# The fourth open PSUM bank of a wide output projection: drawn from the mixers' pool instead of the transposes' pool

## The chip, the cores and the metric

The kernel runs on one core of one Trainium2 chip. The metric is device time in microseconds (us) of one execution. Every time given here comes from the runs of the kernel or from one execution taken with the hardware profiler.

## What is computed

Two layers of a hybrid block over 1024 tokens of width 1024. Each layer normalises its input, projects it into four mixers (a pooling mixer, retention, a spatial gate, a gated delta rule), projects their joined output back, adds the residual, and then runs a convolutional feed-forward part of inner width 2816:

```python
h = rms_norm(x, g_pre_mix)
p = h @ w_in
...
y = jnp.concatenate([y_a, y_b, y_c, y_d], axis=-1).astype(dt)
x = x + rms_norm(y @ w_out, g_post_mix)
h = rms_norm(x, g_pre_ffn)
x = x + rms_norm(conv_ffn(h, ffn_w_up, ffn_conv_w, ffn_conv_b, ffn_w_down), g_post_ffn)
```

The change touches the product `y @ w_out`, the output projection, in three of its four executions.

## The kernel before

**Tiling.** The 1024 tokens are worked off in two halves of 512 (h = 0 and 1), each as four blocks of 128 tokens. Every float32 weight unit (128 x 1024) is loaded on SP's queue into one of two `raw` buffers, rounded to a high part on ScalarE (L183, `whi`) and the remainder taken on VectorE or GpSimd (L184, `wlo`); `whi` and `wlo` have three buffers each. A product is then three TensorE matmuls: high x high, high x low, low x high.

**Order of the stages.** `run` writes them down as: feed-forward of layer 0 half 0, its norms, the transposes of the result (`to_hT`), the output projection of layer 0 half 1 (`out(0, 1)`), the input projection and mixers of layer 1 half 0 (`win(1, 0)`), and so on; one step later the same sequence comes again with `out(1, 0)` and `win(1, 1)`. The third call of the wide projection, `out(1, 1)`, is put into the middle of the feed-forward part of layer 1 half 0 (`mid`). A scheduler then orders the instructions of each engine; every engine works off its own list strictly in that order, and waits on semaphores of the others.

**The wide projection.** `k_outer` (L219 to L234) keeps four PSUM banks open, one per token block b, and runs over the eight weight units `wO` in two column halves q of four units each: for each unit, for each block, two inner steps of three matmuls (L230, L231, L232). So one call of `out` makes 2 x 4 x 4 x 2 x 3 = 192 matmuls of 128x512. After the last unit of a half, ScalarE copies each bank out (L994).

**The PSUM pools.** The eight banks are split into three pools: `psg`, three banks, for the large products; `psh`, two banks, for the transposes of `to_hT` (L363, eight of 128x128 per token block, four to a bank); `psm`, three banks, for the mixers' small products. A pool hands its banks out in the order in which the program text asks for them, and a new tenant waits until the one before it has been read. `k_outer` asks for three banks of `psg` and one of `psh`. In both places where `to_hT(acc)` stands ahead of `out` in `run`, all eight `psh` tenants of the transposes come before the fourth bank of `k_outer`.

**What feeds the transposes.** `norms` (L308 to L320) goes over the four blocks of `acc`: a sum of squares on ScalarE (L305), an inverse root of ten small VectorE steps (L293, L276 to L284), a scaling (L315), the residual added (L316, `xb`, with two buffers, stored by L317 and loaded by L312 on SP's queue), a second sum of squares and inverse root, and a second scaling (L320), whose result is transposed on TensorE (L363) and split into `hT` by ScalarE (L366) and VectorE (L367). `hT` is what `win` multiplies by: its first matmuls are L214 to L216.

Of the kernel before, what the change touches and what calls it, by code (L numbers as in the profile page):

```python
# [115 lines left out]
class Net:  # L116
# [100 lines left out]
            yield b, ps  # L217

    def k_outer(self, aps, hT, kpu):  # L219
        banks = [self.ps(), self.ps(), self.ps(), self.pq("h")]  # L220
        nk = len(hT)
        for i, ap in enumerate(aps):
            hi, lo = self.unit(ap)
            for b in range(NB):
                tb = slice(b * P, b * P + P)
                for kk in range(kpu):
                    k = kpu * i + kk
                    s = slice(kk * 512, kk * 512 + 512)
                    h0, h1 = hT[k][0][:, tb], hT[k][1][:, tb]
                    self.nc.tensor.matmul(banks[b], h0, hi[:, s], start=k == 0, stop=False)  # L230
                    self.nc.tensor.matmul(banks[b], h0, lo[:, s], start=False, stop=False)  # L231
                    self.nc.tensor.matmul(banks[b], h1, hi[:, s], start=False, stop=k == nk - 1)  # L232
                if i == len(aps) - 1:
                    yield b, banks[b]  # L234
# [943 lines left out]
```

## Time and profile before

| what | value |
|---|---|
| median of 3 runs | 2557.17 us (2554.63 to 2559.59) |
| the profiled execution | 2563.22 us, of which its span is 2561.4 us |
| mean granted TensorE clock | 0.979 |
| VectorE busy | 1723.7 us (67%) |
| ScalarE busy | 937.4 us (37%) |
| GpSimd busy | 237.3 us (9%) |
| data moved | 265.54 MB, a mean of 104 GB/s |

The profile's page gives, for one execution, each engine's busy time, a strip of 40 time slices, the chain of work that ended last, and the costliest groups of instructions by source line. Behind it stands the trace, from which single instructions, waits and windows of time are read. PE is TensorE, PEld its weight loads, DVE VectorE, ACT ScalarE, POOL GpSimd, SP the queue that issues most transfers. PEclk is the granted TensorE clock as a share of full speed. A row of the timeline gives start, duration, engine, line, operation, output and input tiles and their count, and in brackets how long the engine stood idle before it and what ended the wait. Matmuls overlap: one of 128x512 is shown with some 0.39 us, but the next starts earlier, and the distance between two starts is what a matmul costs in a dense stretch.

### The profile page before, as it was taken

The numbers are of one execution on the slowest core, as the hardware profiler recorded it, in microseconds if no ns is written. First come the engines' busy times: TensorE is split into PE (matmuls) and PEld (weight loads), VectorE is DVE, ScalarE is ACT, GpSimd is POOL, SyncE is SP. The second block draws the span as 40 slices with busy tenths as digits, with TensorE's granted clock in tenths as the row PEclk, the third lists the DMA queues.
The fourth block names the chain that finished last, engine by engine and source line by source line (L and its number), as shares of the span: only waits on it lengthen the run. The fifth ranks groups of instructions, "written<-read, shape, count | busy, mean of one in ns | idle before, by whom it ended". The sixth has DMA issues, their size and how long they took to land.

```text
span 2561.4 us, 35079 instructions
## 1 busy us (share of the span) xinstructions
PE 2450.8 (96%) x13532; PEld 1998.9 (78%) x13532; DVE 1723.7 (67%) x3553; ACT 937.4 (37%) x1382; POOL 237.3 (9%) x318
## 2 busy tenths in 40 slices
PE   8999898999999799799999979989999999999998
PEld 7878677877788588687778858878777888888886
DVE  8895689765655768966565576896556476655556
ACT  6343452432333345243233334524323243432332
POOL 2321113000000012300000000230000000000001
PEclk9999999999999799999999979999999999999999
DMA  5233342322233343222222334322223244433322
GB/s 182 72 96 109 120 134 85 97 83 75 79 99 117 129 142 116 71 80 87 80 83 92 115 123 147 120 75 80 87 80 99 91 156 139 134 98 99 99 92 90
DMA packets 94651, 265.54 MB, mean 104 GB/s; under 512 B 30146, under 2 KB 30466, under 8 KB 93972
## 3 DMA queue, kind: packets, MB, share of 16 engines
q1 hardware_dynamic: 90564, 251.17, 30.8%
q0 software_dynamic: 3344, 11.08, 1.3%
q8 instruction: 107, 1.75, 0.3%
q10 hardware_dynamic: 576, 1.05, 0.1%
q14 instruction: 60, 0.49, 0.1%
HBM read 241.20 MB, written 22.05 MB: 103 GB/s over the span
## 4 chain that ended last, share of the span: by engine, by line
PE 82%; DVE 12%; issue 3%; ACT 2%; DMA 1%; POOL 1%; SPq 0%; DVEq 0%; POOLq 0%; ACTq 0%
PE psg L194 16%; PE psg L195 16%; PE psg L193 15%; PE psg L1016 6%; PE psg L1017 6%; PE psg L1018 6%; DVE pr L830 3%; PE psg L214 1%; PE psg L215 1%; PE psg L216 1%; DVE A L832 1%; PE psg L230 1%; PE psg L232 1%; PE psg L231 1%; DVE wlo L184 1%
## 5 line engine op out<-in xcount | busy, mean ns | idle before, releaser
L194 PE MATMUL psg<-hT,whi 128*128 128x512 f32 x1856 | 739.5, 398 | 1.8 <-DVE hT L367 1.8
L195 PE MATMUL psg<-hT,wlo 128*128 128x512 f32 x1856 | 738.7, 400 | 0.0
L193 PE MATMUL psg<-hT,whi 128*128 128x512 f32 x1856 | 731.2, 394 | 1.5 <-ACT tmp L430 1.4
L183 ACT CAST whi<-raw 128x1024 fp32r<-128x1024 f32 (+1 forms) x383 | 397.9, 1048 | 858.3 <-PE psg L194 340.8
L184 DVE TENSOR_TENSOR wlo<-raw,whi 128x1024 fp32r<-128x1024 f32 (+1 forms) x360 | 440.1, 1230 | 304.7 <-ACT whi L183 297.6
L193 PEld LDWEIGHTS psg<-hT,whi 128*128 128x128 f32 x1856 | 353.7, 191 | 82.6 <-issue 2.0
L194 PEld LDWEIGHTS psg<-hT,whi 128*128 128x128 f32 x1856 | 350.0, 189 | 83.7 <-DVE hT L367 2.9
L195 PEld LDWEIGHTS psg<-hT,wlo 128*128 128x128 f32 x1856 | 349.8, 188 | 76.1 <-issue 1.2
L1023 DVE TENSOR_TENSOR acc<-acc,psg 128x512 f32<-128x512 f32 x312 | 212.6, 685 | 138.3 <-PE psg L1018 137.0
L1016 PE MATMUL psg<-whi,g 128*128 128x512 f32 x696 | 277.3, 400 | 0.3 <-DVE acc L1023 0.3
L1017 PE MATMUL psg<-wlo,g 128*128 128x512 f32 x696 | 274.1, 394 | 0.0
L1018 PE MATMUL psg<-whi,g 128*128 128x512 f32 x696 | 273.4, 393 | 0.0
L1016 PEld LDWEIGHTS psg<-whi,g 128*128 128x128 f32 x696 | 130.7, 188 | 31.4 <-DVE acc L1023 1.6
L1018 PEld LDWEIGHTS psg<-whi,g 128*128 128x128 f32 x696 | 130.8, 188 | 30.2
L215 PE MATMUL psg<-wlo,hT 128*128 128x256 f32 (+1 forms) x512 | 147.4, 289 | 6.1 <-DVE wlo L184 6.1
L1048 DVE TENSOR_TENSOR c<-c,psg 128x512 f32<-128x512 f32 x88 | 60.5, 688 | 136.6 <-PE psg L195 128.5
L1017 PEld LDWEIGHTS psg<-wlo,g 128*128 128x128 f32 x696 | 130.9, 188 | 27.2 <-DVE c L1048 0.2
L214 PE MATMUL psg<-whi,hT 128*128 128x256 f32 (+1 forms) x512 | 146.4, 288 | 3.7 <-DVE rqk L508 3.4
L216 PE MATMUL psg<-whi,hT 128*128 128x256 f32 (+1 forms) x512 | 146.6, 287 | 0.0
L830 DVE SCALAR_TENSOR_TENSOR pr<-A 64x1 f32<-64x1 f32 (+30 forms) x124 | 113.0, 912 | 7.9 <-POOL A L826 5.6
L1047 ACT ACTIVATE c<-c 128x512 f32<-128x512 f32 x88 | 55.6, 632 | 168.5 <-DVE c L1046 85.8
L215 PEld LDWEIGHTS psg<-wlo,hT 128*128 128x128 f32 x512 | 97.4, 190 | 10.0 <-DVE wlo L184 7.1
(393 smaller groups left out, 3064.7 us busy)
## 6 DMA issues: line engine op xcount, KB each, us to landing
raw<-in_wU SPq DMA_DIRECT2D x176, 512.0 KB, 3.5
raw<-in_wD SPq DMA_DIRECT2D x88, 512.0 KB, 3.6
raw<-in_wA SPq DMA_DIRECT2D x56, 512.0 KB, 3.6
raw<-in_wO SPq DMA_DIRECT2D x32, 512.0 KB, 3.6
raw<-in_wB SPq DMA_DIRECT2D x24, 512.0 KB, 3.5
xs<-xb SPq DMA_DIRECT2D x24, 512.0 KB, 2.8
xb<-xs SPq DMA_DIRECT2D x20, 512.0 KB, 3.6
raw<-in_wS SPq DMA_DIRECT2D x8, 528.0 KB, 3.5
```

Of the source, the lines that this page charges most:

```text
L183: nc.scalar.copy(hi[:, :n], raw[:, :n])
L184: eng.tensor_tensor(lo[:, :n], raw[:, :n], hi[:, :n].bitcast(F32), ALU.subtract)
L193: nc.tensor.matmul(ps, a[0], b[0], start=first, stop=False)
L194: nc.tensor.matmul(ps, a[0], b[1], start=False, stop=False)
L195: nc.tensor.matmul(ps, a[1], b[0], start=False, stop=last)
L215: self.nc.tensor.matmul(ps[:, :width], h0, lo[:, s], start=False, stop=False)
L216: self.nc.tensor.matmul(ps[:, :width], h1, hi[:, s], start=False, stop=k == len(hT) - 1)
L830: V.scalar_tensor_tensor(pr[:, 0:i, 0:i], A[:, 0:i, 0:i], -1.0, A[:, 0:i, i].unsqueeze(1).to_broadcast([64, i, i]), ALU.mult, ALU.mult)
L1016: nc.tensor.matmul(ps, hi[:, tb], us[i][0][:, s], start=i == 0, stop=False)
L1017: nc.tensor.matmul(ps, hi[:, tb], us[i][1][:, s], start=False, stop=False)
L1018: nc.tensor.matmul(ps, lo[:, tb], us[i][0][:, s], start=False, stop=i == len(g0) - 1)
L1023: V.tensor_tensor(acc[b][:, s], acc[b][:, s], ps, ALU.add)
```

## The change

The call that asks for the fourth bank of `k_outer` gets it from `psm` instead of `psh`:

```diff
     def k_outer(self, aps, hT, kpu):
-        banks = [self.ps(), self.ps(), self.ps(), self.pq("h")]
+        banks = [self.ps(), self.ps(), self.ps(), self.pq()]
         nk = len(hT)
         for i, ap in enumerate(aps):
             hi, lo = self.unit(ap)
```

No instruction is added to or removed from the computation; the fourth bank's tenants change, and with them the order in which the scheduler puts the instructions.

**TensorE, first of the two places (`to_hT(acc)` and `out(0, 1)`).** Before, the transposes of all four token blocks (`acc_5206` to `acc_5209`) stood in one row, and behind them the first matmuls into the fourth bank (`psh`); `y_7867` to `y_7870` are the projection's input:

```order
L230 MATMUL psg<-whi,y_7869 128x512
L231 MATMUL psg<-wlo,y_7869 128x512
L232 MATMUL psg<-whi,y_7870 128x512
L363 MATMUL psh<-ident,acc_5206 128x128 x8
L363 MATMUL psh<-ident,acc_5207 128x128 x8
L363 MATMUL psh<-ident,acc_5208 128x128 x8
L363 MATMUL psh<-ident,acc_5209 128x128 x8
L230 MATMUL psh<-whi,y_7867 128x512
L231 MATMUL psh<-wlo,y_7867 128x512
L232 MATMUL psh<-whi,y_7868 128x512
```

In the changed kernel the transposes of a block stand alone between matmuls of the projection; this is the place of the third block:

```order
L230 MATMUL psm<-whi,y_7867 128x512
L231 MATMUL psm<-wlo,y_7867 128x512
L363 MATMUL psh<-ident,acc_5208 128x128 x8
L232 MATMUL psm<-whi,y_7868 128x512
L230 MATMUL psg<-whi,y_7869 128x512
```

Counted over the whole list, 60 of the 192 matmuls now stand ahead of the first block's transposes, then 39, 44 and 47 between one block's and the next, and 2 behind the last; before, 54 stood ahead of the first and 138 behind the last.

**ScalarE, the same place.** Before, the rounding of the fourth and later `wO` units (L183) stood behind the last block's `hT` (L366):

```order
L305 ACTIVATE sq,ss<-xb 128x1024
L366 CAST hT_7807<-psh 128x4x128
L366 CAST hT_7808<-psh 128x4x128
L183 CAST whi<-raw 128x1024 x3
L994 COPY raw_7887<-psg 128x512
```

In the changed kernel roundings and bank copies stand between the sums of squares of the norms (`acc_5208`, `acc_5209` are the third and fourth block):

```order
L305 ACTIVATE sq,ss<-acc_5208 128x1024
L366 CAST hT_7807<-psh 128x4x128
L366 CAST hT_7808<-psh 128x4x128
L183 CAST whi<-raw 128x1024
L994 COPY raw_7887<-psg 128x512
L994 COPY raw_7888<-psg 128x512
L994 COPY raw_7889<-psg 128x512
L183 CAST whi<-raw 128x1024
L305 ACTIVATE sq,ss<-xb 128x1024
L366 CAST hT_7807<-psh 128x4x128
L366 CAST hT_7808<-psh 128x4x128
L305 ACTIVATE sq,ss<-acc_5209 128x1024
```

On SP's queue the loads of later `wO` units move in the same way to between the loads and stores of `xb`. The second place (`out(1, 0)`) has the same changes with other tile numbers. In the third call (`out(1, 1)`, in the middle of the feed-forward part) the rows keep their places, and only the name of the fourth bank changes. Inside `win(1, 0)` and `win(1, 1)` some rows of VectorE and ScalarE change places, and ScalarE loads its function table twice more in each.

## The prediction

> **What bounds the kernel now.** First the page: busy times, then the shares of the chain that ended last.
>
> ```profile
> PE 2450.8 (96%) x13532; PEld 1998.9 (78%) x13532; DVE 1723.7 (67%) x3553; ACT 937.4 (37%) x1382; POOL 237.3 (9%) x318
> PE 82%; DVE 12%; issue 3%; ACT 2%; DMA 1%; POOL 1%; SPq 0%; DVEq 0%; POOLq 0%; ACTq 0%
> ```
>
> TensorE is busy in 96% of the span and carries 82% of the chain. Time can be won only where it stands still or runs at a low clock. So next: for whom does it wait longest in total (us, times, longest)?
>
> ```profile
> PE psh L363 <- DVE rt L281: 21.8, 4, 6.5
> PE psh L363 <- DVE acc L320: 12.5, 2, 6.3
> ```
>
> These are the first and third largest entries of that list, and both are the transposes of `to_hT` waiting for the norms. The timeline of TensorE shows where they lie. First place, `out(0, 1)`:
>
> ```profile
> 848.81 0.39 PE L230 MATMUL psg<-whi,y 128*128 128x512 f32 x1
> ...
> 861.07 0.39 PE L232 MATMUL psg<-whi,y 128*128 128x512 f32 x1
> 861.30 1.04 PE L363 MATMUL psh<-ident,acc 128*128 128x128 f32 x8
> 866.69 1.94 PE L363 MATMUL psh<-ident,acc 128*128 128x128 f32 x8 [4.35 <-DVE rt L281]
> 875.17 1.94 PE L363 MATMUL psh<-ident,acc 128*128 128x128 f32 x8 [6.54 <-DVE rt L281]
> 883.37 1.94 PE L363 MATMUL psh<-ident,acc 128*128 128x128 f32 x8 [6.25 <-DVE acc L320]
> 885.86 0.79 PE L230 MATMUL psh<-whi,y 128*128 128x512 f32 x1 [0.55 <-DVE hT L367]
> 886.45 0.63 PE L231 MATMUL psh<-wlo,y 128*128 128x512 f32 x1
> ...
> 892.00 0.43 PE L232 MATMUL psh<-whi,y 128*128 128x512 f32 x1
> ...
> 920.44 0.39 PE L232 MATMUL psh<-whi,y 128*128 128x512 f32 x1
> 920.66 0.28 PE L214 MATMUL psg<-whi,hT 128*128 128x264 f32 x1
> ```
>
> 54 matmuls of the projection run until the transposes begin at 861.30. Then TensorE has nothing but 32 transposes until 885.86, waiting each time for a block's norms, and the other 138 matmuls follow. They do not depend on the transposes by their data. They stand behind them only because their bank is one of the two that the transposes use. The windows of this stretch give busy time, number and granted clock:
>
> ```profile
> 848.80:861.30 12.50, 12.50 (x55) 10.10 (x54) 10.88 (x28) 4.67 (x7) 0.00 (x0) 1.00 0.53 171
> 861.30:885.90 24.60, 6.91 (x34) 5.54 (x32) 19.31 (x64) 9.38 (x18) 0.00 (x0) 0.57 0.34 125
> 885.90:892.20 6.30, 6.30 (x15) 4.95 (x16) 1.91 (x2) 1.90 (x3) 0.00 (x0) 0.51 0.06 14
> 892.20:920.66 28.46, 28.46 (x124) 23.11 (x124) 7.96 (x16) 10.48 (x15) 2.48 (x1) 1.00 0.37 115
> ```
>
> TensorE's columns are the first after the length. It works 6.91 of 24.60 us, the granted clock falls to 0.57, and it stays at 0.51 for a further 6.3 us. From 886.45 to 892.00 lie 13 starts: 5.55 / 13 = 0.427 us each. Before, from 848.81 to 861.30, they lie 12.49 / 54 = 0.2313 us apart. The second place, `out(1, 0)`, repeats this:
>
> ```profile
> 1494.01 0.39 PE L230 MATMUL psg<-whi,y 128*128 128x512 f32 x1
> ...
> 1506.50 1.04 PE L363 MATMUL psh<-ident,acc 128*128 128x128 f32 x8
> 1511.88 1.94 PE L363 MATMUL psh<-ident,acc 128*128 128x128 f32 x8 [4.35 <-DVE rt L281]
> ...
> 1565.80 0.28 PE L214 MATMUL psg<-whi,hT 128*128 128x264 f32 x1
> ```
>
> **The change, part by part.** From the projection's first matmul to the first of `win` the first place takes 920.66 - 848.81 = 71.85 us, the second 1565.80 - 1494.01 = 71.79 us. What must be done there is 192 matmuls x 0.2313 = 44.4 us and four groups of transposes x 1.04 us (row 861.30, the group at full clock) = 4.2 us: 48.6 us. If nothing waits, each place gives 71.8 - 48.6 = **23.2 us**. This holds the waits, the half clock of the transposes (1.94 against 1.04 us) and that of the 15 matmuls behind them.
>
> Does nothing wait? Each engine keeps its order, so the transposes between the matmuls can hold TensorE up. Six matmuls go ahead into the end of the feed-forward part, which moves that end by 6 x 0.23 = 1.4 us. Then, by the counts of the changed list, the transposes of block 0 come 54 matmuls after 850.2, at 862.7, and the others each 39 to 47 matmuls and 1.04 us later: on average 130 / 3 x 0.2313 + 1.04 = 11.1 us, so at 872.8, 884.0 and 895.9. The norms delivered, before, at the ends of L320:
>
> ```profile
> 855.88 1.29 DVE L320 SCALAR_TENSOR_TENSOR acc<-xb,rs,gpre 128x1024 f32<-128x1024 f32 x1
> ...
> 865.26 1.28 DVE L320 SCALAR_TENSOR_TENSOR acc<-xb,rs,gpre 128x1024 f32<-128x1024 f32 x1
> ...
> 867.23 1.28 DVE L315 SCALAR_TENSOR_TENSOR acc<-acc,rs,gpost 128x1024 f32<-128x1024 f32 x1
> 868.43 0.69 DVE L367 TENSOR_TENSOR hT<-psh,hT 128x512 fp32r<-128x512 f32 x1
> 869.04 1.22 DVE L316 TENSOR_TENSOR xb<-xb,acc 128x1024 f32<-128x1024 f32 x1
> ...
> 870.35 1.06 ACT L305 ACTIVATE sq<-xb 128x1024 bf16<-128x1024 f32 x1 [1.09 <-DVE xb L316]
> ...
> 873.74 1.28 DVE L320 SCALAR_TENSOR_TENSOR acc<-xb,rs,gpre 128x1024 f32<-128x1024 f32 x1
> ...
> 881.93 1.28 DVE L320 SCALAR_TENSOR_TENSOR acc<-xb,rs,gpre 128x1024 f32<-128x1024 f32 x1
> ```
>
> From the second block on that is one block in (881.93 - 865.26) / 2 = 8.3 us, scaling, residual, sum of squares and inverse root one behind the other. Now the splits of six weight units and four bank copies come between. Their prices, in this order on VectorE and ScalarE:
>
> ```profile
> 850.02 1.22 DVE L184 TENSOR_TENSOR wlo<-raw,whi 128x1024 fp32r<-128x1024 f32 x1
> ...
> 888.82 1.04 ACT L183 CAST whi<-raw 128x1024 fp32r<-128x1024 f32 x1 [2.89 <-PE psh L232]
> ...
> 895.62 0.58 ACT L994 COPY raw<-psg 128x512 f32<-128x512 f32 x1
> ```
>
> Per block: two L184 (2.4), two L183 (2.1), 1.3 copies (0.8). If all of it hid, a block took 8.3 us; if all of it lengthened the chain, 13.6 us. I take 10.7 (the L184 alone, since a rounding runs on ScalarE while VectorE is in the inverse root). Block 0 is ready about 1.4 us later than before, at 858.5 (855.88 + 1.29 + 1.4). At 10.7 us a block, block 3 is ready at 890.6, 5 us ahead of its transposes. At 13.6 us it would come at 899.3, 3.4 us late. A rounding also waits for its buffer, which TensorE frees in order: ScalarE stands before the second sum of squares of a block until a unit's last matmul. Counted in the changed list, from that matmul to the block's transposes lie 47 to 70 matmuls and one group of transposes, at least 11.9 us. Against that stand 1.04 for the rounding, 873.74 - 870.35 = 3.4 from the start of the sum of squares to L320, two `hT` splits of 0.69 that may come between, one L184 of 1.22 and 1.28 for L320: 8.3 us. This loop closes in time too. On SP's queue the `xb` loads now stand behind `wO` loads; those wait for `raw` buffers, free at the L184 two units earlier, and a block's `xb` has a round to land.
>
> I therefore take the full 23.2 us twice: **46.4 us**. The third call:
>
> ```profile
> 2065.00:2075.00 10.00, 10.00 (x45) 8.11 (x44) 8.09 (x29) 6.80 (x13) 0.00 (x0) 1.00 0.47 160
> 2075.00:2092.00 17.00, 17.00 (x79) 13.95 (x78) 15.42 (x37) 8.45 (x13) 0.00 (x0) 1.00 0.56 181
> ```
>
> TensorE is full there at clock 1.00 and no row moves: 0.
>
> Does the gain arrive at the end? Behind both places VectorE is nearly full:
>
> ```profile
> 940.00:1000.00 60.00, 58.81 (x309) 47.68 (x309) 54.68 (x151) 35.68 (x55) 14.51 (x15) 0.97 0.43 141
> 1000.00:1100.00 100.00, 85.46 (x604) 73.63 (x603) 88.03 (x154) 24.16 (x33) 27.57 (x23) 0.97 0.23 68
> ```
>
> 54.68 of 60 and 88.03 of 100 us. But that work is made of what `win` produces, and begins when `win` begins. From 848.80 to 920.66 VectorE had 10.88 + 19.31 + 1.91 + 7.96 = 40.1 us of work; the same fits into 48.6 us, at 82%. What may still be open when `win` starts is block 3's two L367 and one L315 and L316 of the next norms, about 4 us (0.69 + 0.69 + 1.28 + 1.22): 0 to 4 us a place. The two extra table loads a place
>
> ```profile
> 966.33 1.28 ACT L724 ACT_TABLE_LOAD   x1
> ```
>
> cost ScalarE 2.6 us in a stretch where it works 35.68 of 60 us: 0 on the path, 2.6 if a bank copy behind them held TensorE. On the other side TensorE loses 1.2 us there now and 3% of its clock (about 1.8 us), which another order may win: up to 3 us a place. I take 0 for these and keep -3 to +6.6.
>
> Sum: the profiled execution took 2563.2 us; 2563.2 - 46.4 = 2516.8. The median of the runs is 6.0 us below that execution, so **2511 us**.
>
> On the clock, the Trainium skill (TensorE: Matmul & The Clock Gate, What's actually happening) says that half rate is the idle state, and some 3.4 us of sustained work lift it. The trace has 0.51 for 6.3 us after the pause. By the rule a wait would cost 3.4 / 2 = 1.7 us of rate, by the rows 15 x (0.427 - 0.2313) = 2.9 us; the 23.2 us, a difference of two stretches of the trace, stays the same.
>
> **The rivals.**
>
> *The norms stretch.* At 13.6 us a block TensorE arrives early at the later transposes, waits 3.4 us and loses 2.9 us of clock at up to two of them: 9 us a place, 18 in all, 2529 us. For it: ScalarE and VectorE work in order, and roundings stand ahead of sums of squares. Against it: the 5 us of slack above. Chance 0.13.
>
> *The mixers absorb it.* The stage behind is set by VectorE and does not start earlier; then the result is 2557, or within a few us. For it: 88 of 100 us busy. Against it: VectorE's rows from 886 to 920 are almost idle (9.9 of 34.8 us), waiting for TensorE. The other case with this result, that the bank doesn't decide the order, is excluded by the new list. Chance 0.05.
>
> *The clock falls with every wait.* If a block took 18 us, TensorE would wait 3 x (18 - 11.1) - 4.2 = 16.5 us and lose 3 x 2.9 us of clock: 25.2 us a place against 23.2 won, slower by 2 us each; at 20 us a block by 8 each: 2573 us. It decides from 17.3 us a block, twice today's 8.3, and ScalarE waiting for TensorE while TensorE waits for the norms could feed it. Against it: all added work in series gives 13.6. The Trainium skill has a rule of this kind (TensorE: Matmul & The Clock Gate, A second HAM failure mode: psum-queue depth-cycling): cycling through PSUM banks leaves short gaps in which the clock is lost again. Here four banks are cycled from 892.20 to 920.66 at clock 1.00. Chance 0.03.
>
> **How the numbers follow.** Forecast 0.79, with its own range of 2505 (3 us more a place) to 2524 (6.6 us less); stretched norms 0.13; absorbed 0.05; clock 0.03. About 0.2%, 5 us, is what a measurement of this kernel can tell from no change. Faster: 0.79 + 0.13 = 0.92; same 0.05; slower 0.03. The range goes from 2504 to 2532, so that it takes in the stretched norms.
>
> **What would show it.** After the change: no wait of L363 on L281 or L320 above 1 us in the two places; clock 1.00 through both; 47 to 49 us from the first `psg` matmul of the projection to L214 (six of its matmuls lie ahead of it); the same distances as now from L214 to the end of `win`. A wait at the third or fourth block's transposes shows the stretched norms; a longer `win` shows the absorption. The forecast is wrong if TensorE's starts spread to 0.427 us inside the projection, or if VectorE enters `win` with a backlog over 4 us.

## The result, and the profile after

The changed kernel takes 2509.97 us (median of 4 runs, 2509.2 to 2515.1), the kernel before 2556.93 us in runs beside it: a ratio of 0.982, with a 95% interval of 0.9803 to 0.9837. That is 47.0 us. The forecast was 2511. The profiled execution of the changed kernel took 2509.2 us, of which its span is 2507.4, at a mean granted clock of 0.988.

From the page after: the busy times, then the shares of the chain of waits.

```profile
PE 2439.9 (97%) x13532; PEld 1993.7 (80%) x13532; DVE 1717.5 (68%) x3553; ACT 940.4 (38%) x1386; POOL 238.4 (10%) x318
PE 78%; DVE 12%; issue 4%; ACT 2%; DMA 2%; POOL 1%; DVEq 0%; SPq 0%; POOLq 0%; ACTq 0%
```

TensorE executes the same 13532 instructions, in 10.9 us less busy time (2450.8 before). So most of the gain is idle time that is gone, and a smaller part is matmuls that no longer run at a low clock. The list of TensorE's waits after, with total, number and longest, now begins with two that stand outside the two places (15.6 and 6.1 us before):

```profile
PE psh L363 <- DVE hT L367: 14.9, 5, 5.9
PE psg L215 <- DVE wlo L184: 8.0, 4, 3.3
```

The waits of the transposes on the norms (L281 and L320, 21.8 and 12.5 us before) are no longer among the largest. TensorE's timeline shows the second place, `out(1, 0)`. The row at 1464.83 belongs to the last three matmuls of the feed-forward part:

```profile
1464.83 0.40 PE L1016 MATMUL psg<-whi,g 128*128 128x512 f32 x1
...
1465.52 0.39 PE L230 MATMUL psg<-whi,y 128*128 128x512 f32 x1
...
1478.03 1.03 PE L363 MATMUL psh<-ident,acc 128*128 128x128 f32 x8
...
1487.91 1.04 PE L363 MATMUL psh<-ident,acc 128*128 128x128 f32 x8
...
1498.94 1.03 PE L363 MATMUL psh<-ident,acc 128*128 128x128 f32 x8
...
1510.66 1.03 PE L363 MATMUL psh<-ident,acc 128*128 128x128 f32 x8
```

No row has a bracket: nothing waits, and each group of transposes has the duration of full clock, 1.03 us, where three of four had 1.94. To see where the rest of the program stands, the whole span is cut where a feed-forward part begins (its first L1016), where its last group of matmuls begins (its last L1016) and where `win` begins (its first L214), at these three again, and where the third feed-forward part begins. So the rows are: everything up to the feed-forward part, the feed-forward part, the first place, `win(1, 0)`, the feed-forward part, the second place, `win(1, 1)`. The windows give length, then busy time and count of TensorE, its weight loads, VectorE, ScalarE and GpSimd, then granted clock, DMA share and GB/s. Before, without the last stretch, which runs to the end:

```profile
0.00:488.75 488.75, 451.13 (x3041) 374.70 (x3042) 397.45 (x961) 210.19 (x322) 97.92 (x128) 0.98 0.36 114
488.75:848.12 359.37, 359.37 (x1935) 286.51 (x1934) 207.70 (x354) 115.81 (x178) 13.07 (x43) 1.00 0.28 91
848.12:920.66 72.54, 54.84 (x228) 44.26 (x227) 40.75 (x111) 26.87 (x40) 2.48 (x1) 0.81 0.36 118
920.66:1138.60 217.94, 202.21 (x1250) 170.48 (x1248) 182.46 (x416) 90.10 (x132) 42.45 (x38) 0.98 0.34 107
1138.60:1493.31 354.71, 354.71 (x1901) 284.79 (x1899) 211.52 (x386) 112.48 (x157) 13.39 (x38) 1.00 0.29 91
1493.31:1565.80 72.49, 54.80 (x229) 44.23 (x228) 40.76 (x111) 26.87 (x40) 2.48 (x1) 0.81 0.36 118
1565.80:1778.99 213.19, 203.24 (x1249) 171.12 (x1248) 178.70 (x400) 90.69 (x136) 42.63 (x29) 0.97 0.34 108
```

The same stretches after:

```profile
0.00:483.29 483.29, 452.26 (x3041) 377.95 (x3042) 392.98 (x961) 210.10 (x322) 99.88 (x128) 0.97 0.36 115
483.29:843.90 360.61, 360.61 (x1941) 287.70 (x1939) 208.51 (x355) 115.82 (x178) 13.07 (x43) 1.00 0.29 91
843.90:891.05 47.15, 47.15 (x222) 38.81 (x221) 37.87 (x108) 25.73 (x40) 2.48 (x1) 1.00 0.58 189
891.05:1108.88 217.83, 204.62 (x1250) 171.91 (x1248) 182.87 (x418) 92.87 (x135) 44.49 (x38) 0.96 0.34 105
1108.88:1464.83 355.95, 355.95 (x1906) 286.01 (x1905) 212.27 (x387) 112.49 (x157) 13.39 (x38) 1.00 0.29 91
1464.83:1512.00 47.17, 47.17 (x222) 38.81 (x221) 37.88 (x109) 25.72 (x40) 2.48 (x1) 1.00 0.58 189
1512.00:1724.96 212.96, 201.66 (x1250) 169.65 (x1248) 180.91 (x402) 93.20 (x139) 39.78 (x29) 0.98 0.34 107
```

The third and sixth rows are the two places. They shrink by 25.39 and 25.32 us and TensorE is busy in all of them at clock 1.00. The feed-forward rows ahead of them grow by 1.24 us each, for the six projection matmuls that went into them. So a place gains 24.15 and 24.08 us. The `win` rows change by -0.11 and -0.23, and the last stretch is as long as before (782.41 and 782.44).

The first row differs by 5.46 us although nothing in it was changed: the engines' lists are the same up to the first place. The executions profiled in this study end this stretch anywhere between 480.2 and 488.8 us, with the same list up to there (one exception, told below). It is scatter, and it is why two single executions differ by 54.0 us and the medians by 47.0.

### The profile page after: what moved, and what is told of

The parts are those of the page before. It is cut to its first block, busy times and chain, and to the rows that moved or that the text cites. A ratio compares the mean times of both kernels' runs of the same rounds, so it can differ in the third digit from the quotient of the medians.

```text
span 2507.4 us, 35082 instructions
## 1 busy us (share of the span) xinstructions
PE 2439.9 (97%) x13532; PEld 1993.7 (80%) x13532; DVE 1717.5 (68%) x3553; ACT 940.4 (38%) x1386; POOL 238.4 (10%) x318
## 4 chain that ended last, share of the span: by engine, by line
PE 78%; DVE 12%; issue 4%; ACT 2%; DMA 2%; POOL 1%; DVEq 0%; SPq 0%; POOLq 0%; ACTq 0%
PE psg L194 15%; PE psg L195 15%; PE psg L193 14%; PE psg L1016 6%; PE psg L1017 6%; PE psg L1018 6%; DVE pr L830 3%; DVE wlo L184 1%; PE psg L230 1%; PE psg L232 1%; PE psg L231 1%; DVE A L832 1%; PE psg L214 1%; PE psg L215 1%; PE psg L216 1%
## 5 line engine op out<-in xcount | busy, mean ns | idle before, releaser
L183 ACT CAST whi<-raw 128x1024 fp32r<-128x1024 f32 (+1 forms) x383 | 398.0, 1048 | 835.7 <-PE psg L194 337.3
L1016 PE MATMUL psg<-whi,g 128*128 128x512 f32 x696 | 277.1, 400 | 0.3 <-DVE acc L1023 0.3
L1016 PEld LDWEIGHTS psg<-whi,g 128*128 128x128 f32 x696 | 130.7, 188 | 30.8 <-DVE acc L1023 1.0
L214 PE MATMUL psg<-whi,hT 128*128 128x256 f32 (+1 forms) x512 | 147.4, 290 | 1.6 <-DVE rqk L508 1.5
```

Source lines behind the costliest of these rows:

```text
L183: nc.scalar.copy(hi[:, :n], raw[:, :n])
L1016: nc.tensor.matmul(ps, hi[:, tb], us[i][0][:, s], start=i == 0, stop=False)
```

## The experiments

**One place alone, and the middle call alone.** The call of `out` says from which pool the fourth bank comes. First, `psm` only in `out(0, 1)`:

```diff
-    def k_outer(self, aps, hT, kpu):
-        banks = [self.ps(), self.ps(), self.ps(), self.pq("h")]
+    def k_outer(self, aps, hT, kpu, src="h"):
+        banks = [self.ps(), self.ps(), self.ps(), self.pq(src)]
...
-                    self.k_outer(aps, yT, 2)
+                    self.k_outer(aps, yT, 2, "m" if (l, h) == (0, 1) else "h")
```

> The kernel before, with the fourth bank from psm in out(0, 1) alone; out(1, 0) and the middle call keep psh. The theory (a place gains what its transposes waited for, each place by itself): 24 us less than before, 2533 us, and the first place takes about 46.5 us from the first psg L230 to the first L214, the second about 71.8 as before. Rival (the gain of the first place is handed on, or the second gains only because the first came early): the whole 47 us or well under 20.

Measured: 2532.32 us, 0.9904 of the kernel before (0.9889 to 0.9919), 24.7 us less. The windows of its two places, cut as above:

```profile
848.43:895.58 47.15, 47.15 (x223) 38.80 (x221) 37.88 (x108) 25.73 (x40) 2.48 (x1) 1.00 0.59 189
1466.46:1538.95 72.49, 54.79 (x228) 44.23 (x227) 40.77 (x111) 26.76 (x40) 2.48 (x1) 0.81 0.36 117
```

The first place is that of the changed kernel, the second that of the kernel before, to the hundredth. Each place gains by itself. (The expectation's 46.5 us for the first place counts from the first `psg` matmul of the projection, 0.69 us behind the start of this window.)

Second, `psm` only in the middle call:

```diff
-                    self.k_outer(aps, yT, 2)
+                    self.k_outer(aps, yT, 2, "m" if mid else "h")
```

> The kernel before, with the fourth bank from psm in the middle call (out(1, 1)) alone. The theory: no transposes stand beside this call and TensorE is full there at clock 1.00, so nothing changes: 2557 us, within 0.2%. Rival (the third psh bank that is left free, or the psm bank that is taken, matters to the feed-forward part around it): over 5 us either way.

Measured: 2557.19 us, a ratio of 1.0002 (0.9992 to 1.0011). The third of the three calls that the change touches adds nothing, as expected.

**The other way round: the transposes move, the fourth bank stays.**

```diff
-    def to_hT(self, hn, wide=False):
+    def to_hT(self, hn, wide=False, src="h"):
...
-                ps = self.ps() if wide and kk == WIDE else self.psh.tile([P, 512], F32, tag="h", name="psh")
+                ps = self.ps() if wide and kk == WIDE else self.pq(src)
...
-            hT = self.to_hT(acc)
+            hT = self.to_hT(acc, src="m")
```

The last edit stands at both places.

> The kernel before, with the fourth bank still from psh, but with the transposes of the two places taken from psm in its place. The theory (what costs is that transposes and fourth bank share one pool, in which the fourth bank stands behind all eight banks of the transposes): as the change, 2510 us, no wait of the transposes on the norms over 1 us. Rival (psm has something of its own to give, such as its three banks or its free time): well above 2510, or as before, 2557.

Measured: 2512.36 us, 0.9827 (0.9813 to 0.9842), and the places take 47.15 and 47.18 us. The three banks of the mixers' pool, or their free time, are not the point: the fourth bank can stay in `psh` if the transposes leave it. What costs is that the two share one pool. Its banks go out in the order of the program text, and there all eight banks of the transposes come first.

**How much of a wait is the clock?** The kernel before, with matmuls that nobody reads in the three waits of each place:

```diff
+            if fill and b:
+                d = self.pq()
+                w = hT[1][:, 0, b * P - P:b * P]
+                for i in range(fill[b - 1]):
+                    nc.tensor.matmul(d, w, self.fr.to_broadcast([P, HALF]), start=True, stop=True)
...
-            hT = self.to_hT(acc)
+            hT = self.to_hT(acc, fill=(13, 22, 22))
```

> The kernel before, with 13, 22 and 22 extra matmuls of 128x512, whose result nobody reads, ahead of the transposes of the second, third and fourth block in both places: TensorE works while it waits for the norms, and nothing else moves. The theory (of the 24 us of a place about 20 are the waits themselves, and the rest is the low clock behind them: 15 x 0.196 = 2.9 us for the matmuls, 0.9 for the last transposes): 3.8 us less a place, 7.6 in all, 2549 us, with clock 1.00 behind the transposes. Rival (the clock is the larger share): 15 us less or more. Rival (the fill costs as much as it wins, since it ends after the norms): 2557 or above.

Measured: 2551.72 us, 0.998 (0.997 to 0.999), 5.3 us less than before (2.6 to 7.7 by the interval). The expected 7.6 lies at its edge; the rival's 15 is excluded. TensorE's timeline at the second place of this kernel (its lines are numbered differently: L370 is the transposes, L365 the fill, L232 to L234 the projection):

```profile
1513.70 1.06 PE L370 MATMUL psh<-ident,acc 128*128 128x128 f32 x8 [0.82 <-DVE rt L283]
1515.50 5.08 PE L365 MATMUL psm<-fr,hT 128*128 128x512 f32 x22 [0.73 <-ACT hT L373]
1522.50 1.07 PE L370 MATMUL psh<-ident,acc 128*128 128x128 f32 x8 [1.93 <-DVE acc L322]
1524.53 0.50 PE L232 MATMUL psh<-whi,y 128*128 128x512 f32 x1 [0.96 <-DVE hT L374]
1524.86 0.39 PE L233 MATMUL psh<-wlo,y 128*128 128x512 f32 x1
```

With TensorE at work the transposes run at full clock, yet the fourth group starts 22.19 us after the first (1500.31 to 1522.50), as in the kernel before (861.30 to 883.37, 22.07). The norms set that distance; the full clock did not shorten it. Behind it the clock stayed full at this place, but at the first place of the same execution, after the same two short waits of 1.93 and 0.96 us, it was low again:

```profile
881.36:890.00 8.64, 7.68 (x30) 6.14 (x31) 3.40 (x4) 3.17 (x4) 0.00 (x0) 0.80 0.22 65
...
1522.50:1531.00 8.50, 7.54 (x36) 6.15 (x37) 3.74 (x4) 3.17 (x4) 0.00 (x0) 1.00 0.35 107
```

The two places took 70.92 and 69.38 us instead of 72.54 and 72.49: 1.6 us were won where the clock fell once more and 3.1 where it did not, against the 3.8 expected of a full clock.

**Are the norms on the path, before and after?** One more pass over `xb` per block, which leaves its value as it is, in the norms of the two places; first in the kernel before:

```diff
                 nc.vector.tensor_tensor(xb, xb, raw[b], ALU.add)
+                for i in range(pad):
+                    nc.vector.scalar_tensor_tensor(xb, xb, 1.0, xb, ALU.mult, ALU.max)
...
-        self.norms(acc, acc, gpost, gpre, src, dst)
+        self.norms(acc, acc, gpost, gpre, src, dst, 0 if last else 1)
```

> The kernel before, with one more VectorE pass of 128x1024 over xb (its own value, some 1.28 us) per block in the norms of the two places. The theory (before, TensorE waits there for the norms' chain, which runs one block behind the other): every pass lengthens the chain and so the place, 4 x 1.28 = 5.1 us a place less what the first block hides (1.3), 3.8 to 5.1, so 8 to 10 us slower, 2565 to 2567 us. Rival (TensorE's wait has another cause, the chain has air): within 3 us of 2557.

Measured: 2570.85 us, 1.0057 (1.0044 to 1.0069): 13.4 us slower, more than the 8 to 10 expected. The transposes wait 7.57, 8.28 and 7.99 us where they waited 4.35, 6.54 and 6.25. The second block comes 3.2 us later behind the first, and the third and fourth 1.7 more each, not 1.22. For these two VectorE's timeline shows why (L369 is the split of `hT`, L318 the added pass):

```profile
870.33 1.22 DVE L316 TENSOR_TENSOR xb<-xb,acc 128x1024 f32<-128x1024 f32 x1
871.46 0.69 DVE L369 TENSOR_TENSOR hT<-psh,hT 128x512 fp32r<-128x512 f32 x1
872.06 1.22 DVE L318 SCALAR_TENSOR_TENSOR xb<-xb 128x1024 f32<-128x1024 f32 x1
```

The second split of the previous block now stands ahead of the pass, inside the chain, 0.6 us. The theory holds, its price was too small; what makes up the 3.2 us of the second block was not taken apart. The same edit in the changed kernel:

> The changed kernel with the same single extra pass per block. The theory (the norms are hidden, block 3 with 5.2 us of slack, and four passes are 5.1): 0 to 1 us, 2510 us, and no wait of the transposes above 1 us. Rival (the norms are still on the path, by what stands between them on VectorE and ScalarE): 8 to 10 us slower as before, 2518 to 2520 us.

Measured: 2500.42 us, 0.9786 (0.9772 to 0.9799). No loss, as the theory had it, and no wait of the transposes in the places. But 9.6 us **less** than the changed kernel (their intervals against the kernel before do not meet) was not foreseen by any theory; the last three experiments return to it. With three passes (`3` in place of `1`):

> The changed kernel with three extra passes per block, 3.84 us. The theory (a slack of about 5 us that is used up, then waits and their low clock): if all of it lengthens a round, block 3 is 15.4 us late against 5.2 of slack, TensorE waits up to 10 us a place and loses up to 3 us of clock: 26 us slower, 2536 us. If the rounds, at 11.0 us, hold 2.7 us a block of waiting that takes up the passes (8.3 in series), a round grows by 1.1 us only and block 3 is 4.6 us late: no change. I expect something between, 2515 to 2530 us, with the waits at the third and fourth blocks. Rival (the transposes between the matmuls can hold TensorE and the norms in a loop, roundings waiting for matmuls and these for the transposes): over 2540 us.

Measured: 2537.24 us, 0.9917 (0.9903 to 0.9932), 27 us slower than the changed kernel. The scheduler, which knows of the passes, put the transposes of the third and fourth blocks behind the start of `win`, and there the fourth's wait. TensorE's timeline, and the window behind the wait:

```profile
905.41 1.94 PE L365 MATMUL psh<-ident,acc 128*128 128x128 f32 x8 [5.51 <-DVE rt L281]
```

```profile
905.41:915.00 9.59, 8.94 (x36) 7.65 (x37) 8.22 (x32) 5.12 (x10) 0.00 (x0) 0.58 0.31 111
```

The clock falls to 0.58, and the whole of `win(1, 0)` takes 230.68 us instead of 217.83 (890.13 to 1120.81), 12.9 more. TensorE is busy 210.92 us in it instead of 204.62, at a mean clock of 0.93 instead of 0.96, so 6.3 us are slower work and the two groups of transposes that came in (some 1.6), and 6.6 us are idle time, most of it this wait. VectorE works 193.34 us there instead of 182.87: 10.5 us that had no room in the place arrive in `win`. How much of the idle time is this backlog, and not the late norms, the run doesn't tell. So the decision point lies between one and three passes a block. My middle estimate, that waiting inside a round would take up part of the cost, was wrong. The worst case, 26 us, fits in its number but only in part in its mechanism: TensorE waits 5.5 us a place, not 10, and the wait stands in `win`. TensorE and the norms don't hold each other in a loop: this is the only wait of the transposes at either place (5.51 us at both).

**The same idea at the other transposes.** After the change TensorE's largest wait is that of the transposes ahead of the feed-forward parts for a bank. Every second block's first bank from `psm`:

```diff
-                ps = self.ps() if wide and kk == WIDE else self.psh.tile([P, 512], F32, tag="h", name="psh")
+                ps = self.ps() if wide and kk == WIDE else self.pq("m" if wide and b % 2 else "h")
```

> The changed kernel, in which the other transposes, those ahead of the feed-forward parts, also take one of two banks of every second block from psm. The theory (their waits for a bank, L363 on L367, 14.9 us in five times, are of the same kind: a pool that is too narrow for its tenants): up to 12 us less, 2498 to 2510 us. Rival (they wait because VectorE, which empties the banks, is full there, so another bank only moves the wait): 2510 us. Rival (the mixers beside them need psm themselves): slower.

Measured: 2764.39 us, 1.0809 (1.0794 to 1.0823), 254 us slower than the changed kernel. Its timeline of TensorE in the second half of `win(0, 1)`, then one window of this kernel, and the same window of the changed kernel:

```profile
558.78 0.66 PE L959 MATMUL psm<-ident,tmp 128*128 128x128 f32 x2 [4.41 <-DVE tmp L615]
559.24 1.91 PE L363 MATMUL psm<-ident,acc 128*128 128x128 f32 x8
```

```profile
430.00:560.00 130.00, 70.97 (x594) 57.08 (x595) 68.89 (x192) 16.70 (x39) 12.27 (x39) 0.50 0.06 13
```

```profile
430.00:560.00 130.00, 129.48 (x719) 104.71 (x718) 92.34 (x174) 48.41 (x75) 4.25 (x10) 0.99 0.28 82
```

In the program text these transposes come behind the mixers, and L959 is the mixers' last use of `psm`. So the transposes now wait for the last mixer, and the feed-forward part behind them, which otherwise runs between the mixers' small products, stands outside: TensorE has 71 us of work in 130, at clock 0.50, with a DMA share of 0.06. This is the mechanism of the kernel before, in the opposite direction and larger. The 12 us that were expected did not come; whether `psh` is too narrow for these transposes this run can't show, since the new order covers it. (Here the first stretch, too, is a changed one: it ends at 613.3 us.)

**Where the 9.6 us of the added pass come from.** The stretches of its execution put 0.84 and 0.88 us in the two places (46.31 and 46.29), where the fourth block's transposes left, and 5.3 us in `win(1, 0)`, 212.57 instead of 217.83. The same pass over a quarter of the width, then over 64 columns, and the changed kernel again:

```diff
-                    nc.vector.scalar_tensor_tensor(xb, xb, 1.0, xb, ALU.mult, ALU.max)
+                    nc.vector.scalar_tensor_tensor(xb[:, :256], xb[:, :256], 1.0, xb[:, :256], ALU.mult, ALU.max)
```

> The changed kernel with the extra pass per block over 128x256 in place of 128x1024, about 0.3 us. The kernel with the full pass came out 9.6 us faster than the changed kernel, 5.3 of it in the window from the first L214 to the feed-forward part in win(1, 0). Theory: the pass itself does nothing for the time; it alters what the scheduler believes, and the order that results, nearly the same here, waits less in win(1, 0): 2500 us, and that window about 212.5 us against 217.8. Rival (the delay itself helps, by spreading work): between, about 2508. Rival (it was scatter of executions): 2510.

> The same with the pass over 128x64, of which the chip hardly feels anything. Its list of TensorE differs from that of the full pass in more rows than the last. Theory (order decides, by chance): anything from 2498 to 2515, different from the others where its list differs in win(1, 0). Rival (the delay decides): as the changed kernel, 2510.

> The changed kernel once more, beside the two, on the same chip. 2510 us, and in its execution the two places at about 47.2 us and win(1, 0) at 217.8. If win(1, 0) comes out at 213 here, the difference to the kernel with the pass is scatter.

Measured: 2511.33 us for a quarter (0.9826, 0.9812 to 0.9841), 2504.14 for 64 columns (0.9794, 0.9778 to 0.9811), 2512.97 for the changed kernel itself (0.9832, 0.9816 to 0.9847). The interval of the 64 columns lies below that of the changed kernel beside it, and overlaps that of its first measurement (0.9803 to 0.9837). The places take 46.3 us in both kernels with a pass and 47.16 in the changed one. One window each over `win(1, 0)`, of the full pass, the quarter, the 64 columns and the changed kernel again:

```profile
887.11:1099.68 212.57, 203.04 (x1257) 171.14 (x1256) 182.47 (x425) 93.72 (x136) 42.34 (x38) 0.98 0.35 110
```

```profile
890.76:1109.02 218.26, 205.66 (x1257) 173.08 (x1256) 183.92 (x429) 89.12 (x132) 39.85 (x38) 0.97 0.35 109
```

```profile
891.73:1101.94 210.21, 200.47 (x1239) 169.67 (x1238) 179.22 (x427) 90.58 (x134) 49.45 (x38) 0.98 0.36 113
```

```profile
893.04:1109.34 216.30, 202.84 (x1250) 171.03 (x1248) 182.71 (x418) 92.83 (x135) 44.14 (x38) 0.98 0.34 106
```

The gain does not grow with the pass: the largest and the smallest have it, the middle one has not. My expectation for the quarter, 2500 us from a similar list, was wrong; the delay as a cause falls with it. Scatter does not explain it either: the changed kernel's two executions have 217.83 and 216.30 us in this window. What is left is the order in which `win` comes out of the scheduler, which these edits shuffle: the rows of VectorE stand there in another order in each of the four kernels, and the window takes 210 to 218 us. That the order does it is argued, not shown; which rows decide was not taken apart. Two of these kernels, the full pass and the 64 columns, are faster than both kernels of this case.

## Why the prediction was right

**The bound.** TensorE's waits in the two places were the thing to win, and the fourth bank in the pool of the transposes was their cause: undoing it in one place gives that place back alone (24.7 us), and undoing it from the side of the transposes gives the whole.

**The sum.** 23.2 us a place were predicted, and 24.15 and 24.08 came. The term that was mis-sized is the four groups of transposes. I gave each its duration in the row, 1.04 us; in a dense stretch one takes less, as TensorE's timeline after shows:

```profile
889.71 1.03 PE L363 MATMUL psh<-ident,acc 128*128 128x128 f32 x8
890.50 0.48 PE L231 MATMUL psm<-wlo,y 128*128 128x512 f32 x1
```

The next matmul starts 0.79 us later, so four groups cost 3.2 us instead of 4.2. The matmuls had been priced by their distance; the transposes should have been, too. This also puts the distance from the first `psg` matmul of the projection to L214 at 46.5 us (844.59 to 891.05), just below the 47 to 49 named as a sign.

**The norms keep up.** Predicted: rounds of 10.7 us, and 5 us of slack at the fourth block. VectorE's timeline after:

```profile
850.33 1.28 DVE L320 SCALAR_TENSOR_TENSOR acc<-xb,rs,gpre 128x1024 f32<-128x1024 f32 x1
...
859.96 1.28 DVE L320 SCALAR_TENSOR_TENSOR acc<-xb,rs,gpre 128x1024 f32<-128x1024 f32 x1
...
871.83 1.28 DVE L320 SCALAR_TENSOR_TENSOR acc<-xb,rs,gpre 128x1024 f32<-128x1024 f32 x1
...
883.20 1.28 DVE L320 SCALAR_TENSOR_TENSOR acc<-xb,rs,gpre 128x1024 f32<-128x1024 f32 x1
```

Rounds of 9.6, 11.9 and 11.4 us, a mean of 11.0. The last block is ready at 884.48, 5.2 us ahead of its transposes at 889.71; the others have 4.9 to 5.7. That the slack came out to 0.2 us is luck in part: the first block was ready 7.0 us behind the projection's first matmul (844.59 to 851.61), not 8.3, and the rounds took 0.8 us more in all. What fills a round is not VectorE's splits alone, as I had priced it. ScalarE's timeline has the loop that the prediction described, a rounding that waits for TensorE, and a second sum of squares behind it:

```profile
866.46 1.05 ACT L183 CAST whi<-raw 128x1024 fp32r<-128x1024 f32 x1 [0.79 <-PE psm L232]
867.41 1.05 ACT L305 ACTIVATE sq<-xb 128x1024 bf16<-128x1024 f32 x1
```

That loop closes in time, as predicted. The stretched norms, the first rival, were a question of a few us a block: one pass (1.22 us) is hidden, three (3.7 us) are not.

**The gain arrives.** `win` kept its length (-0.11 and -0.23 us), so no backlog and no cost of the two table loads shows. The second rival, that the mixers absorb the gain, falls. The three passes come nearest to it: with 10.5 us more VectorE work in `win`, it grew by 12.9, though a wait of TensorE and a low clock have their share in that. The prediction took 0 for what another order of `win` may do, and at most 3 us won a place. That it came out at 0 was luck: the kernel with the pass over 64 columns has 210.21 us in `win(1, 0)`, 7.6 less.

**The clock.** It was 1.00 through both places, with four banks cycled in turn, so the rival of a clock that falls with every wait did not come; nothing waited, and its price was not tested. Of the prediction's 2.9 us for the low clock behind a pause, one thing has to be taken back: that is one draw. The last section shows it.

**From execution to median.** The forecast subtracted 6.0 us for an execution above the median. That execution owed part of it to the first 489 us; the changed kernel's execution lay 0.8 us below its median. With 46.4 priced and 48.2 gained in the pair of traces, the medians moved by 47.0, and by 44.0 in the repetition. So a forecast that lies 1 us from the median is nearer than these figures allow to foresee.

## What to carry to other kernels

Where a pool hands out its tiles in program order, two users of one pool are tied together in that order, even if their data have nothing to do with each other; look for independent work that stands in a row behind waiting work, and ask whose tile it waits for. Whether another pool helps depended here on who asks ahead of it in the program text: to take transposes to the mixers' pool won some 45 us at the two places and lost 254 at the transposes ahead of the feed-forward parts. And where a scheduler orders the rest, a change of no consequence may move a later stage by several us, so the term of a sum is to be tested in its own window, not in the total alone.

## What was not expected of the hardware

**The low clock behind a pause has no fixed length.** Before, 13 starts of 0.427 us lay behind the last transposes of the first place. In the kernel with `psm` in the middle call alone, whose first place has the same list, TensorE's timeline is

```profile
882.75 0.63 PE L231 MATMUL psh<-wlo,y 128*128 128x512 f32 x1
...
885.31 0.41 PE L231 MATMUL psh<-wlo,y 128*128 128x512 f32 x1
885.56 0.39 PE L232 MATMUL psh<-whi,y 128*128 128x512 f32 x1
```

The second row is the sixth start behind the first (2.56 / 6 = 0.427 us each), and the next matmul follows in 0.25 us: the low clock ends some 3 us earlier, and the place is 71.11 us long instead of 72.54, with waits of the same length to within 0.01 us. The windows of the low clock, of the kernel before and of this one:

```profile
864.75:892.05 27.30, 12.02 (x39) 9.54 (x40) 18.70 (x55) 8.68 (x14) 0.00 (x0) 0.50 0.27 97
```

```profile
861.43:885.33 23.90, 8.98 (x32) 7.19 (x33) 17.11 (x49) 7.16 (x13) 0.00 (x0) 0.50 0.32 110
```

The difference is 3.4 us, and the two lengths are 8 and 7 times 3.41. In the kernel before, the clock falls at the second place at 1509.87, 645.12 us behind 864.75, which is 189 times 3.413. So in these traces the clock changes on a grid of 3.41 us, and where a pause falls on the grid decides how long the low clock lasts. In the kernel with the fill it was none at one place and eight starts at the other. The Trainium skill (TensorE: Matmul & The Clock Gate, What's actually happening) says that the window over which activity is judged runs freely and that therefore one kernel shows 6, 11 or 14 slow matmuls, depending on where its start falls. The traces here agree, and show it behind a pause in the middle of a kernel. Behind the waits of the kernel before, the slow matmuls cost 2.9 us where there are 13 starts and about half of that where there are six; behind the shorter waits of the fill, 0 to some 1.6 us (8 x 0.196).
